# Order of weight casts, a scan product, the last sums and the output rows in a two-layer hybrid decoder trunk

## The chip, the cores and the metric

The kernel is one program on one core of a Trainium2 chip. The core has five engines, each with its own instruction queue: TensorE (PE; its weight loads are a row of their own, PEld), VectorE (DVE), ScalarE (ACT), GpSimd (POOL) and SyncE (SP), which here only issues DMAs. An engine works its queue in order, and an instruction waits in its queue until what it needs is there. The metric is device time in microseconds (us) from the first to the last instruction of one launch; lower is better.

## What is computed

`x` has 512 positions of width 1024. There are two layers, each a "macaron": half a SwiGLU feed-forward (FFN), a mixer, half a SwiGLU again, each on an RMS-normalised input. The mixer is a Mamba-2 SSD in layer 0 and an S5 state space model in layer 1. A last RMSNorm gives the output.

```python
for i in range(2):
    x = x + 0.5 * swiglu(rmsnorm(x, ffn1_norm[i]), ffn1_w_in[i], ffn1_w_out[i])   # inner width 2816
    h = rmsnorm(x, mix_norm[i])
    x = x + (ssd_mixer(h, ...) if i == 0 else s5_mixer(h, ...))
    x = x + 0.5 * swiglu(rmsnorm(x, ffn2_norm[i]), ffn2_w_in[i], ffn2_w_out[i])
return rmsnorm(x, final_norm)
```

The S5 mixer has 64 groups of 16 channels with 64 complex states each: a product into the states, a linear recurrence over time, a product back, a gelu, and a gated linear unit (GLU) with a 1024 x 2048 weight. Everything is float32.

## The kernel before

**Stages.** `STAGES` is `f1_0`, `ssd`, `f2_0`, `f1_1`, `s5`, `f2_1`. The residual is kept transposed, eight tiles `xT[0..7]` of 128 channels x 512 positions. `f1_0` uses `ffn`; the other three feed-forwards use `ffn7`.

**Three products for one.** Each fp32 operand is split into a rounded high half and the rest: ACT casts the high half (`whi`, L226), DVE subtracts to get the low half (`wlo`, L228), and `proj` (L235 to L237) adds high x high, high x low and low x high in PSUM. `split_w` does both halves of a weight tile; `split(j)` calls it for the j-th weight of an `ffn7` stage, `fetch_to(j)` sends its DMA on SP.

**The end of an `ffn7` stage.** The 22 blocks of the inner width are worked in five parts, and after each part eight output tiles d = 0..7 are accumulated (`part`, 15 matmuls of 512 columns for a part of five blocks). `after(d)` then adds the product to the residual on DVE (L594 or L597, here "the add of tile d"), and in the last part starts the next norm: `nxt.take(d)` has ACT square the tile (L160) and, where the next stage is a feed-forward, make its high half `hH` (L173); `rest` has DVE make `hL` (L182) and add the square to `acc` (L167). `rest` of tile d is held in `held` until tile d+1. After the last tile, `nxt.sums()` sums `acc` and the last square over the partitions on PE (L198 for S5, L137 otherwise), and `finish()` runs the Newton iterations for 1/sqrt on DVE (L121 to L128). For the last stage, `fin_sink` has ACT scale a tile (L1592); its `rows` turns it on PE (L1597) and copies it to `fo` on DVE (L1598). At most three `rows` wait in `later`; `flush` runs them.

**Lists of work between.** `fill` holds functions that `ffn7` calls one by one, one after each block and after each `after(d)`. In `f1_1`, entries 54 to 61 fall to d = 0..7 and the last, 62, behind them. They load what the S5 stage needs, and `res_w(j)` casts the first four GLU weights (ACT L1381, DVE L1389; weight j loaded by `res_load(j)`, L1375).

**Order.** `tc.manual_schedule(engines=...)` keeps the named engines in the order of the program; where nothing is named, a planner places an engine's instructions by its own simulation of the times. Inside `ffn7` nearly everything is in program order on all engines (`ALL`), but each call is a region of its own; the planner may still place instructions of one region among those of the next. In `s5_stage` PE, SP and POOL are in program order, DVE and ACT are the planner's.

**The S5 stage** works eight blocks of eight groups. `states(i)` scales the input tile `U` by the norm on DVE (L1407) and multiplies it into PSUM on PE (L1413); `swap(i)` copies it half by half on ACT (L1424, L1425); `scan(i)` is eight steps on DVE (L1433 to L1445, with the recurrence at L1437) with two ACT copies in the middle (L1441, L1442) and gives `v`. `mix(i, h, 128)` and `mix(i, h, 0)` multiply `U` and `v` of blocks i and i+1 back (L1454). `channels(i)` turns and splits the gelu's result (L1474 on PE, L1478 on ACT, L1479 on DVE), and `glu_k(k)` accumulates its part of the first four GLU columns, which needs `res_w(0..3)`. `aux` PSUM has four slots, `mm` four.

**The output.** Each of four blocks of 128 rows is scaled by the norm (ACT L1767 or DVE L1765) and sent as one DMA (L1768).

## Time and profile before

| | |
|---|---|
| median of 3 runs | 2044.01 us (2043.23 to 2044.3) |
| profiled execution: its own time | 2039.9 us |
| its span, first to last instruction | 2038.0 us |
| mean granted TensorE clock | 0.991 of full speed |
| busy: PE, PEld, DVE, ACT, POOL | 1988.1, 1727.5, 1493.7, 943.4, 223.9 us |
| PE waiting, named waits above 1 us each, between 1500 and 1700 us | 22.7 us |
| DMA | 265.47 MB, mean 130 GB/s |

The profile is of one execution. A row of its timeline has the start, the duration, the engine, the line of the kernel, the operation, output and inputs, and in brackets how long the engine sat idle before it and what ended that. Matmuls overlap, so their durations are longer than their spacing.

### The profile page before, as it was taken

To read this page: it belongs to the slowest core of one execution; us is meant where nothing else is said; L and a number is where in the kernel's file an instruction comes from. 1 tells how busy PE (TensorE), PEld (TensorE's weight loads), DVE (VectorE), ACT (ScalarE), POOL (GpSimd) and SP (SyncE) were. 2 spreads that over 40 slices of the span, in tenths; PEclk is the share of its full clock that TensorE was granted. 3 is DMA by queue.
4 is the path that set the end of the run, shared out by engine and by line. 5 is a ranking of instruction groups with operands and counts; after the bars stand their busy time and mean duration, and the time that the engine had idled before them with its cause. 6 is when DMAs were issued, how large, how long until landed. Compare 5 with 4: busy or idle time off the path is not lost. (4 is left out here: it accounts for less than half of the span.)

```text
span 2038.0 us, 32117 instructions
## 1 busy us (share of the span) xinstructions
PE 1988.1 (98%) x12477; PEld 1727.5 (85%) x12477; DVE 1493.7 (73%) x2677; ACT 943.4 (46%) x1613; POOL 223.9 (11%) x338
## 2 busy tenths in 40 slices
PE   8999999999999999999999999999996999999997
PEld 7887778888888887889999978999985888999996
DVE  6899995688885787776677677677768657866675
ACT  5324334465663555434444534454444433444453
POOL 1002332012111010000111000001101100100010
PEclk9999999999999999999999999999997999999999
DMA  7436676344333332455566336446767432654561
GB/s 183 127 120 170 161 193 136 93 113 125 110 107 112 99 93 62 115 133 119 138 152 151 86 92 157 114 124 147 177 184 259 134 95 80 163 136 114 129 142 66
DMA packets 410057, 265.47 MB, mean 130 GB/s; under 512 B 40008, under 2 KB 383088, under 8 KB 409904
## 3 DMA queue, kind: packets, MB, share of 16 engines
q1 hardware_dynamic: 383024, 202.60, 35.5%
q0 software_dynamic: 26560, 59.75, 14.1%
q8 instruction: 98, 1.61, 0.3%
q10 hardware_dynamic: 320, 1.06, 0.1%
q14 instruction: 55, 0.45, 0.1%
HBM read 215.06 MB, written 21.04 MB: 116 GB/s over the span
## 5 line engine op out<-in xcount | busy, mean ns | idle before, releaser
L226 ACT CAST whi<-wst 128x1024 fp32r<-128x1024 f32 (+3 forms) x354 | 315.5, 893 | 373.7 <-PE mm L236 290.6
L228 DVE TENSOR_TENSOR wlo<-wst,whi 128x1024 fp32r<-128x1024 f32 (+3 forms) x354 | 364.1, 1029 | 120.8 <-ACT whi L226 119.0
L235 PE MATMUL mm<-hH,whi 128*128 128x512 f32 x984 | 389.9, 396 | 0.0
L236 PE MATMUL mm<-hL,whi 128*128 128x512 f32 x984 | 384.8, 391 | 1.8 <-DVE hL L182 1.7
L237 PE MATMUL mm<-hH,wlo 128*128 128x512 f32 x984 | 383.8, 390 | 0.0
L237 PE MATMUL mm<-ah,wlo 128*128 128x512 f32 x704 | 274.8, 390 | 0.0
L235 PE MATMUL mm<-ah,whi 128*128 128x512 f32 x704 | 274.5, 391 | 0.0
L236 PE MATMUL mm<-al,whi 128*128 128x512 f32 x704 | 274.4, 390 | 0.0
L236 PEld LDWEIGHTS mm<-hL,whi 128*128 128x128 f32 x984 | 185.1, 188 | 40.8 <-DVE hL L182 3.0
L235 PEld LDWEIGHTS mm<-hH,whi 128*128 128x128 f32 x984 | 185.0, 188 | 39.8 <-issue 1.8
L237 PEld LDWEIGHTS mm<-hH,wlo 128*128 128x128 f32 x984 | 185.0, 188 | 39.5 <-issue 0.4
L384 PE MATMUL mm<-th,hH 128*128 128x256 f32 x612 | 173.5, 284 | 0.0
L386 PE MATMUL mm<-th,hL 128*128 128x256 f32 x612 | 173.2, 283 | 0.0
L385 PE MATMUL mm<-tl,hH 128*128 128x256 f32 x612 | 173.1, 283 | 0.0
L237 PEld LDWEIGHTS mm<-ah,wlo 128*128 128x128 f32 x704 | 132.2, 188 | 28.0 <-issue 0.6
L236 PEld LDWEIGHTS mm<-al,whi 128*128 128x128 f32 x704 | 132.3, 188 | 26.5 <-issue 0.2
L235 PEld LDWEIGHTS mm<-ah,whi 128*128 128x128 f32 x704 | 132.3, 188 | 26.1
L299 POOL DMA_DIRECT2D wu<-wst x51 | 43.1, 846 | 827.5 <-DMA wst<-in_ffn_w_in_dram 384.4
L384 PEld LDWEIGHTS mm<-th,hH 128*128 128x128 f32 x612 | 117.4, 192 | 2.4 <-ACT up L458 2.4
L385 PEld LDWEIGHTS mm<-tl,hH 128*128 128x128 f32 x612 | 117.4, 192 | 0.0
L386 PEld LDWEIGHTS mm<-th,hL 128*128 128x128 f32 x612 | 117.4, 192 | 0.0
L385 PE MATMUL mm<-tl,whi 128*128 128x256 f32 x408 | 115.5, 283 | 0.0
(393 smaller groups left out, 3917.6 us busy)
## 6 DMA issues: line engine op xcount, KB each, us to landing
wst<-in_ffn_w_in_dram SPq DMA_DIRECT2D x125, 512.0 KB, 4.6
wu<-in_ffn_w_in_dram SPq DMA_DIRECT2D x51, 512.0 KB, 5.9
wst<-in_ssd_in_proj_dram SPq DMA_DIRECT2D x48, 512.0 KB, 4.0
wst<-in_ffn_w_out_dram SPq DMA_DIRECT2D x72, 256.0 KB, 2.9
wst<-in_ffn_w_out_dram SPq DMA_DIRECT2D x48, 320.0 KB, 3.2
wu<-wst POOLq DMA_DIRECT2D x51, 256.0 KB, 4.5
ws<-wst POOLq DMA_DIRECT2D x51, 256.0 KB, 4.8
dec<-d_cs POOLq DMA_DIRECT2D x16, 512.0 KB, 4.8
```

The lines of the kernel that those rows point to most:

```text
L226: S.copy(hi, st)
L228: V.tensor_tensor(lo, st, hi.bitcast(F32), op=OP.subtract)
L235: PE.matmul(ps, hi[:, k], H[k], start=first and k == 0, stop=False)
L236: PE.matmul(ps, hi[:, k], L[k], start=False, stop=False)
L237: PE.matmul(ps, lo[:, k], H[k], start=False, stop=last and k == n - 1)
L299: G.dma_start(dst, src, accum_op=OP.add)
L384: PE.matmul(ps[:, c0], hi[:, k], mh, start=first and k == 0, stop=False, skip_group_check=True)
L385: PE.matmul(ps[:, c0], hi[:, k], ml, start=False, stop=False, skip_group_check=True)
L386: PE.matmul(ps[:, c0], lo[:, k], mh, start=False, stop=k == 3, skip_group_check=True)
```

## The change

- `split` becomes `high` (fetch and ACT cast) and `low` (DVE subtraction). In the last part of an `ffn7` stage the ACT cast of a coming weight is issued ahead of the tile's square as before, but its DVE subtraction comes behind the add of the tile; at d = 0 and 1 one weight each is cast, so two by d = 1 where there was one.
- In `f1_1`, `rest` of tile 6 (its square into `acc`) comes ahead of the add of tile 7.
- After the last tile, all but the last `rows` are flushed, then the sums are issued, then the last `rows`.
- `res_w(3)` leaves the `fill` list of `f1_1` and stands in `s5_stage` behind `scan(1)`, where ACT and DVE are the planner's.
- `states(3)` is issued ahead of `mix(0, h, 0)`.
- `f2_0` and `f1_1` together lie in one region that keeps all engines in program order.
- The last two of the eight final tiles are copied from PSUM by ACT.
- The output is scaled and sent in eight blocks of 128 half rows (128 x 512): n = 1, 4, 7 scaled and issued by ACT, the other five scaled by DVE and issued by SP.

```diff
-    def split_w(st, kt):
+    def split_hi(st, kt):
         hi = wpool.tile([128, KD, 128], F32R, name="whi", bufs=3)[:, :kt]
         S.copy(hi, st)
+        return hi
+
+    def split_lo(st, hi, kt):
         lo = wpool.tile([128, KD, 128], F32R, name="wlo", bufs=3)[:, :kt]
         V.tensor_tensor(lo, st, hi.bitcast(F32), op=OP.subtract)
         return hi, lo
...
+        halves = {}
+
+        def high(j):
+            if j < len(items) and j not in whole and j not in halves:
+                fetch_to(j)
+                halves[j] = split_hi(raws[j], items[j][1])
+
+        def low(j):
+            if j in halves:
+                whole[j] = split_lo(raws[j], halves.pop(j), items[j][1])
...
-                def after(d):
+                def after(d, j=None):
                     pops(1)
+                    if d == KD - 1 and last and turn:
+                        held.pop(0)()
...
                     if last:
                         held.append(nxt.take(d, hold=True))
-                        if d:
+                        low(j)
+                        if len(held) > 1:
                             held.pop(0)()
...
-                        split(j + 2)
-                        fetch_to(j + 5)
+                        if not last:
+                            split(j + 2)
+                            fetch_to(j + 5)
                         for e in range(2):
-                            after(e)
+                            high(j + 2 + e)
+                            if e == 0:
+                                fetch_to(j + 5)
+                            after(e, j + 2 + e)
                         continue
                     part(d, 0, n)
-                    if d < KD - 1 or last:
+                    if last:
+                        high(j + 2)
+                    elif d < KD - 1:
                         split(j + 2)
                     fetch_to(j + 5)
-                    after(d)
+                    after(d, j + 2)
...
+            nxt.flush(1)
+            if nxt.kind != "hilo":
+                nxt.sums()
             nxt.flush()
             if nxt.kind != "hilo":
-                nxt.sums()
                 nxt.finish()
...
             scan(1)
+            res_w(3)
...
             states(2)
+            states(3)
             for h in range(2):
                 mix(0, h, 0)
-            states(3)
...
-            V.tensor_copy(fin["o"][:, :, d * 128:(d + 1) * 128], p.rearrange("p (t c) -> p t c", t=4))
+            o, pv = fin["o"][:, :, d * 128:(d + 1) * 128], p.rearrange("p (t c) -> p t c", t=4)
+            if d < KD - 2:
+                V.tensor_copy(o, pv)
+            else:
+                S.copy(o, pv)
...
             elif s in s5_pre:
+                region.enter_context(tc.manual_schedule(engines=ALL))
                 with tc.manual_schedule(engines=MAN):
...
-                fill = [lambda: None] * 63
+                fill = [lambda: None] * 62
...
-                fill[62] = lambda: res_w(3)
...
                          have=have, turn=lambda: s5["op"].tile([128, T], F32, name="xn", bufs=1))
+                region.close()
             else:
...
-    for t in range(4):
-        if t % 2:
-            V.tensor_scalar(fin["o"][:, t], fin["o"][:, t], prep.y4[:, t:t + 1], None, op0=OP.mult)
+    for n in range(8):
+        t, cs = n // 2, slice(n % 2 * 512, n % 2 * 512 + 512)
+        o, y, dst = fin["o"][:, t, cs], prep.y4[:, t:t + 1], out[0, t * 128:(t + 1) * 128, cs]
+        if n % 3 == 1:
+            S.activation(o, o, AF.Copy, scale=y)
+            nc.scalar.dma_start(dst, o)
         else:
-            S.activation(fin["o"][:, t], fin["o"][:, t], AF.Copy, scale=prep.y4[:, t:t + 1])
-        (nc.sync, nc.scalar)[t % 2].dma_start(out[0, t * 128:(t + 1) * 128, :], fin["o"][:, t])
+            V.tensor_scalar(o, o, y, None, op0=OP.mult)
+            nc.sync.dma_start(dst, o)
```

More of the change, by code (lines that the diff above doesn't have):

```diff
@@ L229, in split_w @@
         return hi, lo
+    def split_w(st, kt):
+        return split_lo(st, split_hi(st, kt), kt)
     def proj(ps, w, H, L, first=True, last=True):
@@ L327, in fetch_to @@
                 raws.append(fetch_w(*items[len(raws)])[0])
+        halves = {}
[6 more added lines that the diff above has]
+                whole[j] = split_lo(raws[j], halves.pop(j), items[j][1])
         def split(j):
-            if j < len(items) and j not in whole:
-                fetch_to(j)
-                whole[j] = split_w(raws[j], items[j][1])
+            high(j)
+            low(j)
         sevens = list(range(parts[0][1], FT))
@@ L599, in after @@
                         held.append(nxt.take(d, hold=True))
-                        if d:
+                        low(j)
+                        if len(held) > 1:
                             held.pop(0)()
@@ L1597, in rows @@
                 PE.transpose(p[:, t * 128:(t + 1) * 128], xg[:, t * 128:(t + 1) * 128], ident)
-            V.tensor_copy(fin["o"][:, :, d * 128:(d + 1) * 128], p.rearrange("p (t c) -> p t c", t=4))
+            o, pv = fin["o"][:, :, d * 128:(d + 1) * 128], p.rearrange("p (t c) -> p t c", t=4)
[3 more added lines that the diff above has]
+                S.copy(o, pv)
         return rows
-    op_es = ExitStack()
+    op_es, region = ExitStack(), ExitStack()
     def prep_for(st):
```

## The prediction, made before the changed kernel was run

> **What bounds the kernel now.** I read the page first: the busy shares and the two rows of slices for PE and its clock.
>
> ```profile
> PE 1988.1 (98%) x12477; PEld 1727.5 (85%) x12477; DVE 1493.7 (73%) x2677; ACT 943.4 (46%) x1613; POOL 223.9 (11%) x338
> PE   8999999999999999999999999999996999999997
> PEclk9999999999999999999999999999997999999999
> ```
>
> PE is the bound nearly everywhere. The exceptions are slice 30 (1528 to 1579 us), the S5 scans, where the clock falls too, and the last slice. Work on DVE or ACT is worth something only where PE or the end waits for it, so I asked next for PE's waits: first at the join of `f2_0` and `f1_1` (1100 to 1300), then around S5 (1480 to 1720).
>
> ```profile
> PE mm L236 <- DVE hL L182: 1.4, 1, 1.4
> ...
> PE aux L1454 <- DVE v L1445: 12.4, 4, 4.9
> PE aux L1413 <- DVE U L1407: 5.8, 1, 5.8
> PE aux L1454 <- issue: 2.3, 1, 2.3
> PE aux L198 <- POOL v L1440: 2.2, 1, 2.2
> ```
>
> Together with the output's tail, these places are all that this change can shorten; the other weight casts that it moves stand beside a PE that waits for nothing. The sum is made against the profiled execution, 2039.9 us (span 2038.0, 1.9 around it); it lies 4.1 below the median of 2044.0. I subtract the gain from the median.
>
> **Term 1, the join of f2_0 and f1_1.** Timeline of DVE and PE:
>
> ```profile
> 1179.76 0.69 DVE L597 SCALAR_TENSOR_TENSOR xT<-mm,xT 128x512 f32<-128x512 f32 x1
> 1181.62 1.22 DVE L228 TENSOR_TENSOR wlo<-wst,whi 128x1024 fp32r<-128x1024 f32 x1
> 1182.75 0.75 DVE L182 SCALAR_TENSOR_TENSOR hL<-xT,cols,hH 128x512 fp32r<-128x512 f32 x1
> 1183.55 0.50 PE L236 MATMUL mm<-hL,whi 128*128 128x512 f32 x1 [1.42 <-DVE hL L182]
> ```
>
> PE waits 1.42 for the last `hL`, which stands behind a weight subtraction that begins 1.13 earlier (1181.62 to 1182.75). That subtraction is `f1_1`'s own third weight, put ahead by the planner. One region over both stages forbids it: -1.13 alone. With the adds ahead of the subtractions, the add at 1179.76 also comes sooner, so the whole wait goes: **-1.4** (ends 0 and -1.4). Next late would be tile 6's `hL`, now done before PE asks. The displaced subtraction serves a weight that is used behind two whole projections of 24 matmuls, which cover it; uncovered it would cost its 1.22. SP's order is the same in both programs.
>
> **Term 2, the sums before S5.** Timeline of the end of `f1_1`, DVE, ACT, PE:
>
> ```profile
> 1527.15 0.79 DVE L167 TENSOR_TENSOR acc<-acc,sq 128x512 f32<-128x512 f32 x1
> 1528.57 1.29 DVE L1389 TENSOR_TENSOR hL<-wst,hH 128x512 fp32r<-128x512 f32 x2 [0.63 <-ACT hH L1381]
> 1532.51 1.29 DVE L1389 TENSOR_TENSOR hL<-wst,hH 128x512 fp32r<-128x512 f32 x2 [2.64 <-ACT hH L1381]
> 1533.72 0.22 DVE L121 TENSOR_SCALAR nw_v<-aux 128x64 f32<-128x64 f32 x1
> 1536.87 2.50 DVE L1407 TENSOR_TENSOR U<-U,nw_y 128x512 f32<-128x512 f32 x4
> ...
> 1527.40 0.63 ACT L160 ACTIVATE sq<-xT 128x512 f32<-128x512 f32 x1 [0.84 <-DVE xT L594]
> 1531.86 1.14 ACT L1381 CAST hH<-wst 128x512 fp32r<-128x512 f32 x2 [2.80 <-DMA wst<-in_s_glu_w_dram]
> ...
> 1528.05 1.97 PE L198 MATMUL aux<-acc,sel 128*128 128x64 f32 x16 [2.16 <-POOL v L1440]
> 1529.85 1.95 PE L198 MATMUL aux<-sq,sel 128*128 128x64 f32 x16
> ```
>
> PE is free at 1525.89 (1528.05 less 2.16) and starts when `acc` holds tile 6 (1527.15 + 0.79 = 1527.94). The wait's named releaser, a POOL memset, is not what the code makes it wait for. With tile 6's square ahead of the add of tile 7, and the adds no longer behind subtractions, `acc` is ready before PE is. The 1.80 of the first sums (1528.05 to 1529.85) then falls into the wait for the last square, done at 1528.03; the second sums run 1528.05 to 1530.0. The Newton steps, though, started only at 1533.72, behind `res_w(3)`, whose weight landed at about 1531.8. With `res_w(3)` gone they start at 1530.05; `res_w(2)` (done 1529.86) still fits before. That is **-3.7**. The ends: -0 if something takes `res_w(3)`'s place, -3.7. I take the latter, since in the program nothing stands between the sums and Newton.
>
> `res_w(3)` itself, two ACT casts (1.14) and two DVE subtractions (1.29), is not saved. It has room on ACT under Newton, and on DVE behind the first two of the four scalings of `U` (1536.87, 0.6 each), where 1.48 stood idle before 1540.84 (below). I take 0; without that cover it is +1.2 on DVE.
>
> **Term 3, the fourth scan product.** PE, then DVE, then groups of DVE lines between 1530 and 1600, then SP:
>
> ```profile
> 1568.86 1.73 PE L1454 MATMUL aux<-opP,v 128*64 128x128 f32 x13 [2.81 <-DVE v L1445]
> 1572.11 1.13 PE L1454 MATMUL aux<-opP,v 128*64 128x128 f32 x15
> ...
> 1540.84 0.69 DVE L1433 TENSOR_TENSOR z<-aux,tb 128x512 f32<-128x512 f32 x1 [1.48 <-ACT z L1425]
> 1560.22 0.69 DVE L1433 TENSOR_TENSOR z<-aux,tb 128x512 f32<-128x512 f32 x1 [3.44 <-ACT z L1425]
> ...
> L1433 DVE TENSOR_TENSOR z<-aux,tb 128x512 f32<-128x512 f32 x8 | 5.5, 687 | 5.9 <-ACT z L1425 5.9
> L1444 DVE TENSOR_TENSOR z<-z,tb 128x504 f32<-128x504 f32 x8 | 5.4, 680 | 1.3 <-ACT z L1442 1.1
> ...
> 1539.63 0.32 SPq L1340 DMA_DIRECT2D opH<-d_H  x1
> ```
>
> In this stretch DVE sets the pace: PE's four waits at L1454 are for its `v`. DVE itself idles 3.44 before scan 3, because `states(3)` stood behind `mix(0, h, 0)`, which waited for scan 1. Issued ahead, it needs the PSUM slot that scan 1's first step frees, `U(3)` (scaled by 1539.4), and an operator whose DMA SP issues at 1539.63. DVE then goes from scan 2 into scan 3 without the gap, and PE's resumption at 1568.86, after which it hardly waits again, moves with it: **-3.4** (ends 0 and -5.9, all of L1433's idle). `mix(0, h, 0)` now queues behind `states(3)`; it waited for scan 1 anyway. SP and POOL keep their order.
>
> **Term 4, the tail.** DVE, ACT, PE, and one microsecond of the windows (DMA share, GB/s last):
>
> ```profile
> 2024.67 2.48 DVE L1598 COPY fo<-aux 128x512 f32<-128x512 f32 x4
> 2027.06 0.15 DVE L121 TENSOR_SCALAR nw_v<-aux 128x4 f32<-128x4 f32 x1
> 2029.50 1.42 DVE L1765 TENSOR_SCALAR fo<-fo,nw_y 128x1024 f32<-128x1024 f32 x2
> 2024.25 0.63 ACT L160 ACTIVATE sq<-xT 128x512 f32<-128x512 f32 x1 [2.63 <-DVE xT L597]
> 2030.29 0.37 ACTq L1768 DMA_DIRECT2D out_dram<-fo  x1
> 2026.13 0.43 PE L137 MATMUL aux<-ones,acc 128*32 128x1 f32 x32
> 2026.40 0.44 PE L137 MATMUL aux<-ones,sq 128*32 128x1 f32 x32
> 2031.00:2032.00 1.00, 0.00 (x0) 0.00 (x0) 0.00 (x0) 0.69 (x1) 0.00 (x0) 0.50 0.89 348
> ```
>
> The sums take 0.71 and can start after the last square (2024.88): done at 2025.65. DVE has two copies left instead of four, 0.6 each, free at about 2025.9. Newton starts there instead of 2027.06: -1.15. The two copies on ACT run beside Newton's 2.44 (2027.06 to 2029.50). Half rows are scaled some 0.35 sooner than whole ones (1.42 / 2 = 0.71 for a whole one), so the first DMA leaves that much sooner: -0.35. Data flows from about 2031.1, 0.8 behind that issue, at 348 GB/s in 0.89 of a microsecond, 391; 2.1 MB at that rate take 5.4, as before, and the last issue comes well within that. Term 4 is **-1.5** (ends -0.5, if smaller transfers flow worse, and -1.7).
>
> Beside this stands a rule that speaks against it. The Trainium skill, "DMA: Bandwidth & Descriptors", section "Anatomy of one DMA", gives each DMA about 2.0 us fixed plus its bytes at 436 GB/s; one after another, eight transfers of 256 KB would be 21 us where four of 512 KB are 13, an estimate from that page that would make this term +6.5. The window above, at 391 GB/s with several in flight, speaks against taking them singly.
>
> **Sum:** -1.4 - 3.7 - 3.4 - 1.5 = -10.0, so 2034.0 us (2029.9 for an execution like the profiled one).
>
> **Rivals.** *Newton stays blocked (2037.7).* `res_w(3)` is now the planner's to place. If its simulation has the weight landing early, DVE gets those subtractions into the small hole before Newton (1529.86 to 1530.05) and waits for the real landing at 1531.8: term 2 is gone, 2044.0 - 6.3. For it: four scalings of `U` already run well ahead of their place in the program. Against it: Newton is ready almost at once.
>
> *The S5 gains are swallowed (2041.1).* If DVE's new order, or loads that cannot come sooner, give back terms 2 and 3, only 1.4 + 1.5 = 2.9 stay. For it: one load waited on a full queue in this stretch.
>
> ```profile
> 1559.11 6.89 SPq L1340 DMA_DIRECT2D opH<-d_H  x1
> ```
>
> Against it: that load is for blocks used 20 us later.
>
> *The clock too (2032.7).* The windows show PE at 0.50 from 1566 to 1572, after a wait of 2.81:
>
> ```profile
> 1568.00:1569.00 1.00, 0.14 (x2) 0.17 (x4) 1.00 (x3) 0.96 (x3) 0.00 (x0) 0.50 0.97 381
> ...
> 1582.51 1.04 PE L1454 MATMUL aux<-opP,v 128*64 128x128 f32 x16
> ```
>
> The products from 1568.86 to 1573.24, three groups of thirteen to fifteen, took 4.4; sixteen at full clock take 1.04, so 3.1 for three. If the shorter wait keeps the clock up, 1.3 more goes. The Trainium skill, "TensorE: Matmul & The Clock Gate", section "What's actually happening", says that a free-running window of 3.4 us decides, so a mostly idle window halves the clock and a busy one restores it; the halved stretch here, about two such windows, agrees. Against it: DVE would then be late again.
>
> *The drain (2039.6).* If each of the eight transfers showed its 0.8 of start-up, where one shows it now, 5.6 would be added. For it: smaller pieces. Against it: the rate with four in flight.
>
> *Slower (2050).* The planner stops weaving the scans.
>
> ```profile
> 1565.57 0.61 ACT L1441 COPY z<-z 64x504 f32<-64x504 f32 x1 [1.74 <-DVE z L1437]
> ```
>
> Each scan has two pauses of two such copies on ACT, 2.4 in all, 19.5 for eight (an estimate from this row), of which 7.2 are paid now (5.9 + 1.3 above). Bare, they cost +12.3, against -6.6 from terms 1, 2 and 4: +5.7. It turns slower once the bare pauses pass 13.8 in all, about six of the eight scans. For it: DVE and ACT are free here and their inputs move. Against it: the weave now leaves only 7.2.
>
> **How the numbers follow.** Chances: forecast 0.41, Newton blocked 0.25, swallowed 0.16, clock 0.07, drain 0.02, slower 0.09. About 4 us (0.2%) is what a measurement of this kernel can tell from no change. Faster: 0.41 + 0.25 + 0.07 + 0.02 = 0.75; same 0.16; slower 0.09. The range from 2031.5 (clock case, and a little of L1433's other idle) to 2041.5 (swallowed) leaves out the slower case and some of each end.
>
> **What would show it.** Right: no wait at L236 near 1180; Newton's first step within 0.2 us of the sums' end; `states(3)` directly behind `states(2)` and no 3 us gap before scan 3; Newton at the end about 2.4 us behind the last add, and output at 400 GB/s. Wrong: L1389 between the sums and Newton, DVE idle inside the scans above 7 us, PE's waits at L1454 still near 12, or output below 300 GB/s. The blocked rival would show in the DVE order alone; the slower one only in many short waits for ACT.

## The result and the profile after

The changed kernel is faster: median 2032.69 us (2031.72 to 2034.68, 4 executions) beside 2043.62 for the kernel before (2040.74 to 2044.3, 4 executions), a ratio of 0.995 with a 95% interval of 0.9934 to 0.9966. The forecast was 2034.0 with a range of 2031.5 to 2041.5. The profiled execution took 2032.91 (span 2031.1), 6.9 less span than the profiled one of before. The medians differ by 10.9. Those two differences do not agree, and most of the experiments go into that.

The page's busy shares and the rows of slices, the same three as before:

```profile
PE 1987.0 (98%) x12477; PEld 1727.1 (85%) x12477; DVE 1493.0 (74%) x2678; ACT 944.6 (47%) x1616; POOL 225.6 (11%) x338
PE   8999999999999999999999999999996999999997
PEclk9999999999999999999999999999997999999999
```

Nothing is to be seen at this scale. PE is busy 1.1 us less, and slice 30 still reads 6. The waits of PE, from 1480 to 1720, changed in kind (engine, line, releaser: us in total, times, longest):

```profile
PE aux L1481 <- DVE v L1472: 7.5, 4, 3.7
PE aux L1440 <- DVE U L1434: 6.8, 1, 6.8
PE aux L1440 <- issue: 2.6, 1, 2.6
PE aux L1481 <- issue: 1.5, 1, 1.5
PE aux L1501 <- ACT gy L1489: 0.7, 1, 0.7
PE mm L242 <- DVE hL L182: 0.3, 1, 0.3
```

Lines have moved by 27 in the S5 stage: L1481 is the old L1454 (products back), L1440 the old L1413 (`states`), L1472 and L1471 the old L1445 and L1444 (`v`), L1460 the old L1433 (first step of a scan), L1416 and L1408 the two halves of `res_w`. The wait for `v` fell from 12.4 to 7.5, and the 2.2 ahead of the sums is gone. Others are new or longer: 1.0 more for `U`, 2.6 at `states`, 0.7 for `gy`. All in all 19.4 against 23.0 (the 22.7 of the table before, and a 0.3 for `hL` that stood there too).

**The join.** DVE's timeline at the end of `f2_0`, then the first and the last of seven starts of PE there now, and the first, second and last of the same seven before:

```profile
1179.02 0.75 DVE L182 SCALAR_TENSOR_TENSOR hL<-xT,cols,hH 128x512 fp32r<-128x512 f32 x1
1180.28 0.75 DVE L182 SCALAR_TENSOR_TENSOR hL<-xT,cols,hH 128x512 fp32r<-128x512 f32 x1
1180.94 1.22 DVE L231 TENSOR_TENSOR wlo<-wst,whi 128x1024 fp32r<-128x1024 f32 x1
...
1181.16 0.39 PE L241 MATMUL mm<-hH,whi 128*128 128x512 f32 x1
1182.61 0.43 PE L137 MATMUL aux<-ones,acc 128*32 128x1 f32 x32
...
1180.68 0.39 PE L235 MATMUL mm<-hH,whi 128*128 128x512 f32 x1
1181.15 0.50 PE L236 MATMUL mm<-hL,whi 128*128 128x512 f32 x1
1184.22 0.43 PE L137 MATMUL aux<-ones,acc 128*32 128x1 f32 x32
```

The last `hL` now stands ahead of the weight subtraction (L231), and PE has no wait at all between 1100 and 1300. The six matmuls ahead of the sums (L137) take 1.45 from start to start (1181.16 to 1182.61) where they took 3.54 (1180.68 to 1184.22).

**The end of f1_1.** Timeline of DVE, ACT and PE:

```profile
1530.00 0.69 DVE L1416 TENSOR_TENSOR hL<-wst,hH 128x512 fp32r<-128x512 f32 x1 [2.05 <-ACT hH L1408]
1530.61 0.22 DVE L121 TENSOR_SCALAR nw_v<-aux 128x64 f32<-128x64 f32 x1
1530.74 0.68 DVE L1416 TENSOR_TENSOR hL<-wst,hH 128x512 fp32r<-128x512 f32 x1
1531.34 0.19 DVE L122 TENSOR_SCALAR nw_h<-nw_v 128x64 f32<-128x64 f32 x1
1529.35 1.14 ACT L1408 CAST hH<-wst 128x512 fp32r<-128x512 f32 x2 [2.20 <-DMA wst<-in_s_glu_w_dram]
1524.13 1.89 PE L198 MATMUL aux<-acc,sel 128*128 128x64 f32 x16
1526.17 2.00 PE L198 MATMUL aux<-sq,sel 128*128 128x64 f32 x16
```

The sums start without a wait and end at 1528.17. The Newton steps (`nw_v`) could start there, but start at 1530.61: DVE stood 2.05 us at a subtraction of `res_w(3)`, whose weight had not landed (ACT's cast of it waited 2.20 for the DMA). The second half of the same subtraction cuts in behind Newton's first step. This is what the forecast called "Newton stays blocked", here for 2.4 us.

**The scans.** The two groups of DVE that had 5.9 and 1.3 us of idle time before (between 1530 and 1600; here between 1527 and 1594), then two rows of DVE's and one of PE's timeline:

```profile
L1460 DVE TENSOR_TENSOR z<-aux,tb 128x512 f32<-128x512 f32 x8 | 5.5, 685 | 2.2 <-ACT z L1452 2.2
L1471 DVE TENSOR_TENSOR z<-z,tb 128x504 f32<-128x504 f32 x8 | 5.4, 681 | 2.5 <-ACT z L1469 2.4
...
1543.06 0.68 DVE L1460 TENSOR_TENSOR z<-aux,tb 128x512 f32<-128x512 f32 x1
1554.26 0.68 DVE L1460 TENSOR_TENSOR z<-aux,tb 128x512 f32<-128x512 f32 x1
1543.84 1.15 PE L1440 MATMUL aux<-U,opH 128*64 128x64 f32 x32 [2.62 <-issue]
```

Scan 3 starts at 1554.26 with no idle time before it, where 3.44 stood. `states(3)` (1543.84) waits 2.62 on PE. The profile names no releaser; it starts 0.1 behind the end of scan 1's first step (1543.06 + 0.68), which frees the PSUM slot that it needs by the code. L1460's idle fell by 3.7 and L1471's grew by 1.2, so 2.5 net.

**The tail.** DVE, ACT, SP, and two of the microseconds of output (share of DMA and GB/s last), then two of those of the kernel before:

```profile
2019.17 1.28 DVE L1628 COPY fo<-aux 128x512 f32<-128x512 f32 x2
2020.37 0.15 DVE L121 TENSOR_SCALAR nw_v<-aux 128x4 f32<-128x4 f32 x1
2020.74 0.59 ACT L1630 COPY fo<-aux 128x512 f32<-128x512 f32 x1 [0.28 <-PE aux L1625]
2023.36 3.74 SPq L1804 DMA_DIRECT2D out_dram<-fo  x5
...
2025.00:2026.00 1.00, 0.00 (x0) 0.00 (x0) 0.00 (x0) 0.00 (x0) 0.00 (x0) 0.50 1.00 367
2026.00:2027.00 1.00, 0.00 (x0) 0.00 (x0) 0.00 (x0) 0.00 (x0) 0.00 (x0) 0.50 1.05 387
...
2033.00:2034.00 1.00, 0.00 (x0) 0.00 (x0) 0.00 (x0) 0.00 (x0) 0.00 (x0) 0.50 1.01 393
2034.00:2035.00 1.00, 0.00 (x0) 0.00 (x0) 0.00 (x0) 0.00 (x0) 0.00 (x0) 0.50 1.02 410
```

Newton starts behind two copies, ACT does the other two beside it, and eight transfers of 256 KB flow at 367 to 387 GB/s in the four whole microseconds of output. The four of 512 KB before flowed at 393 to 410 (2032 to 2036), so the smaller ones are about 6% slower, some 0.35 us for the 2.1 MB (an estimate from these rates).

**A ruler for small effects.** Executions of one kernel differ by several us, more than most of the terms. Each stage that ends in a norm has a first Newton step (`nw_v`), and the times between these split an execution into pieces, of which only those that an edit touches should move. In the table, the columns are the first Newton step behind `f2_0`'s start, the length from there to the steps of `f1_1`, S5, `f2_1` and the last norm, and from there to the end:

| kernel | start | f2_0 and join | f1_1 | S5 | f2_1 | end | span |
|---|---|---|---|---|---|---|---|
| before | 837.18 | 349.18 | 347.36 | 148.32 | 345.02 | 10.94 | 2038.0 |
| before, run again | 835.63 | 349.13 | 348.76 | 148.80 | 345.02 | 10.96 | 2038.3 |
| changed | 837.66 | 347.10 | 345.85 | 145.93 | 343.83 | 10.73 | 2031.1 |
| changed, run again | 836.25 | 347.09 | 345.81 | 145.91 | 343.82 | 10.72 | 2029.6 |

The pieces repeat within 0.1 us, but for two in the kernel before (f1_1 and S5) and the start, which moves by 1.4 to 1.6 in either kernel. In the kernel before that is a half clock of 3.4 us from 790 on (1.7 us lost), which all of the fourteen profiles of this document show but the second one of before; in the kernel changed both profiles have it, and the 1.4 is not explained. From the first row to the third: +0.5 - 2.1 - 1.5 - 2.4 - 1.2 - 0.2 = -6.9.

### The profile page after: what moved, and what is told of

The parts are those of the page before. It is cut to its first block, busy times and chain, and to the rows that moved or that the text cites. A ratio compares the mean times of both kernels' runs of the same rounds, so it can differ in the third digit from the quotient of the medians.

```text
span 2031.1 us, 32128 instructions
## 1 busy us (share of the span) xinstructions
PE 1987.0 (98%) x12477; PEld 1727.1 (85%) x12477; DVE 1493.0 (74%) x2678; ACT 944.6 (47%) x1616; POOL 225.6 (11%) x338
## 4 chain that ended last, share of the span: by engine, by line
PE 57%; DVE 2%; ACT 1%; issue 1%; DMA 0%; DVEq 0%; SPq 0%; ACTq 0%
PE mm L241 10%; PE mm L242 10%; PE mm L243 10%; PE mm L400 6%; PE mm L401 6%; PE mm L402 6%; PE aux L402 2%; PE aux L401 2%; PE aux L400 2%; DVE z L1464 0%; PE aux L242 0%; PE aux L243 0%; PE aux L241 0%; DMA wst<-in_s_glu_w_dram 0%; PE aux L1481 0%
## 5 line engine op out<-in xcount | busy, mean ns | idle before, releaser
L231 DVE TENSOR_TENSOR wlo<-wst,whi 128x1024 fp32r<-128x1024 f32 (+3 forms) x354 | 363.9, 1028 | 98.6 <-ACT whi L226 96.8
L615 DVE SCALAR_TENSOR_TENSOR xT<-mm,xT 128x512 f32<-128x512 f32 x112 | 77.1, 688 | 65.4 <-PE mm L243 65.3
```

The source lines that it names most:

```text
L231: V.tensor_tensor(lo, st, hi.bitcast(F32), op=OP.subtract)
L615: V.scalar_tensor_tensor(xT[d], pos[d], 0.5, xT[d], op0=OP.mult, op1=OP.add)
```

## The experiments

All comparisons have five rounds. The median, the range and the count of executions are of the kernel named; the ratio is to the kernel before, run beside it. The comparisons were made in three sets, by the record on three different chips, so differences between medians of different sets say less than the ratios and the pieces.

### Does the kernel before have one time?

**The kernel before, unchanged, as a kernel of its own** (no edit).

> The kernel before, unchanged, as a second look. Between the two profiled executions the change gains 6.9 us of span (2038.0 to 2031.1), between the medians 10.9 (2043.62 to 2032.69). Theory A: the executions of before simply scatter, its profiled one (2039.9) lies at the fast end, and no stage of its own explains the difference: a second profile has the same waits within 0.5 us each, and the median over more runs comes out at 2041 to 2043, so that the change is worth 8 to 9. Theory B: the slower executions of before have one place that is longer (the S5 stage, where PE waits and the granted clock halves): a second profile near 2043 would show 3 to 4 us more in the waits at the scans than the first, and the median stays at 2043 to 2044.

Measured: 2040.55 (2039.0 to 2043.69, 11), ratio 0.9998 [0.9989, 1.0007]. The bound of 0.2% for what counts as a change holds. The median lies below what either theory gave, that of the 25 executions beside it (2041.52) in the range of theory A. The single times are not spread evenly, though. As the other side of the comparisons of all the sections here, the kernel before ran 66 times: 34 executions lie between 2037.62 and 2041.56 (median 2040.05), 32 between 2042.57 and 2044.30 (median 2043.45), none between. The step is 3.4. Of the eleven executions of this section, eight lie in the lower group, two in the upper one, and one (2042.16) in the gap, so the gap is thin but not empty. The execution profiled first (2039.9) is of the lower group, the median of 2044.01 that the forecast subtracted from is of the upper.

In this run's profile the sums of `f1_1` took nearly twice the 1.97 and 1.95 shown before (PE, then DVE):

```profile
1526.42 3.65 PE L198 MATMUL aux<-acc,sel 128*128 128x64 f32 x16 [2.16 <-POOL v L1440]
1529.86 3.62 PE L198 MATMUL aux<-sq,sel 128*128 128x64 f32 x16
1533.52 0.22 DVE L121 TENSOR_SCALAR nw_v<-aux 128x64 f32<-128x64 f32 x1 [1.86 <-PE aux L198]
```

Newton then waits for the sums (1.86) and no longer for `res_w(3)`. So the granted clock had halved in the 2.16 wait ahead of the sums in this execution, and not in the first. S5, where theory B looked for the difference, is 0.5 longer here, not 3 to 4.

### The join

**The region alone.** The kernel before with `f2_0` and `f1_1` in one region, nothing else.

```diff
             elif s in s5_pre:
+                region.enter_context(tc.manual_schedule(engines=ALL))
...
+                region.close()
```

> Before, with f2_0 and f1_1 in one region that keeps all engines in program order, and nothing else. Theory A (the planner's early subtraction alone made PE wait for the last hL): the wait of 1.42 falls to 0.3 or less, 1.1 to 1.4 us faster (ratio 0.9993 to 0.9995). Rival B (the adds ahead of the subtractions did it): the wait stays above 1, no change. If the region also moves other work in the planner's order, the time may differ by several us either way.

Measured: 2036.8 (2035.69 to 2037.56, 9), ratio 0.9975 [0.9965, 0.9984]. The wait at the join falls to 0.30 and the piece "f2_0 and join" to 348.0, 1.2 less, both as expected. The median is 4.7 less than that of before beside it, which misses the expected 1.1 to 1.4 and is more than the wait can give. Its nine executions lie within 1.9 of each other, with no second group.

**The wait kept, and filled.** In the kernel before, six matmuls whose result nobody uses are put where PE waits for `hL`.

```diff
+                        hi, lo = whole[0]
+                        proj(pg, (hi[:, :7], lo[:, :7]), pr.H[:7], pr.L[:7], last=False)
+                        idle = aux_ps()
+                        for n in range(6):
+                            PE.matmul(idle, hi[:, n], pr.H[n], start=n == 0, stop=n == 5)
+                        proj(pg, (hi[:, 7:], lo[:, 7:]), pr.H[7:], pr.L[7:], first=False)
```

> Before, with six extra matmuls of 512 columns (1.4 us by the 0.23 spacing; their PSUM is never read) put into PE's wait for the last hL at the join of f2_0 and f1_1. The wait is filled, not removed; nothing downstream starts earlier. Theory A (a wait of this length lets the granted clock halve in part of the executions, 3.4 us lost each time, as in the profile of the fourth-product run at 1183 to 1191): the median falls by 1.5 to 3.4 us against before although no wait is gone (ratio 0.9985 to 0.9993), and no execution shows a halved clock at the join. Rival B (the join costs its 1.4 of waiting and nothing else, and the region's 4.7 came from another order of work): no change, or up to 0.3 us slower.

Measured: 2039.73 (2037.73 to 2041.35, 11), ratio 0.9992 [0.9983, 1.0001]. The wait still costs its time (the piece is 349.14), the lowest times are those of before, and the upper group is gone: 0 of 11. The interval of the ratio reaches 1, so it is the missing group, more than the median, that speaks for theory A.

**Both waits filled**, the join's and the 2.16 ahead of the sums, with nine more such matmuls there.

```diff
+                for n in range(9):
+                    PE.matmul(idle, h[:, n % 5], AH[n % 5], start=n == 0, stop=n == 8)
             if nxt.kind != "hilo":
                 nxt.sums()
```

> Before, with extra matmuls in two waits: six at the join of f2_0 and f1_1, nine (2.1 us) ahead of the sums before S5. Nothing starts earlier by itself. Theory A (the clock halves in these two waits in part of the executions): the sums take 1.9 to 2.0 a half in every execution instead of up to 3.65, no halved stretch stands at the join, the median falls to 2038 to 2039.5, near the fastest executions of before (2037.6), and none is above 2041. Rival B (the scatter of before is loads landing late): spread and median as before, 2040.5 to 2042.

Measured: 2039.51 (2038.28 to 2041.08, 11), ratio 0.999 [0.9981, 0.9998]. Again none of the upper group: with the run before, 0 of 22, where the kernel before has 32 of 66. The sums take 1.97 and 1.95 in its profile, where they took 2.52 and 3.62 with the join's wait alone filled. By the medians, filling that second wait gives nothing on top (2039.51 beside 2039.73); by the pieces f1_1 is 0.8 shorter (346.81 beside 347.60), and no more, since Newton then stands behind `res_w(3)`.

What the upper group is can be read where a profile happened to catch the clock at the join. Single microseconds there (PE's busy time and matmuls first, the granted clock third from the right), of the fourth product alone (below):

```profile
1182.00:1183.00 1.00, 0.00 (x0) 0.00 (x0) 1.00 (x2) 0.00 (x0) 0.00 (x0) 1.00 0.37 111
1183.00:1184.00 1.00, 0.94 (x11) 0.43 (x14) 0.00 (x1) 0.37 (x1) 0.00 (x0) 0.74 0.30 81
1184.00:1185.00 1.00, 1.00 (x65) 0.98 (x65) 0.29 (x1) 0.68 (x1) 0.00 (x0) 0.50 1.09 329
...
1189.00:1190.00 1.00, 1.00 (x4) 0.81 (x3) 0.00 (x0) 0.00 (x0) 0.00 (x0) 0.50 0.02 6
```

and of the kernel before, run again:

```profile
1184.00:1185.00 1.00, 1.00 (x7) 0.80 (x6) 0.96 (x3) 0.00 (x0) 0.00 (x0) 1.00 0.38 102
1189.00:1190.00 1.00, 1.00 (x8) 0.87 (x7) 0.00 (x0) 0.53 (x1) 0.00 (x0) 1.00 0.00 0
```

The same wait of 1.4 us halves the clock behind it in one execution (full matmuls fall from 6 to 8 a microsecond to 4) and not in the other. From 1183 to 1191 the loss is 3.4 us of full clock, summed from the rows (1 less the clock in each): the step between the two groups. The execution profiled for `res_w(3)` alone (below), at 2042.7 in the upper group, also has the clock at 0.50 there, and in these two profiles the f1_1 piece is 350.79 and 350.84, 3.4 more than the 347.36 of the first profile. That the wait at the join can cost 3.4 us is shown by these two profiles, and that it makes the upper group, by the 22 executions in which filling it removes that group.

The traces also show much of what decides in a single execution. In each of them the granted clock changes only at moments that lie whole multiples of 3.41 us apart. In the first profile it is halved from 1534.54 to 1541.37, from 1548.19 to 1558.43 and from 1565.26 to 1572.09: two, three and two times 3.41, with two times 3.41 between them. (In a row of one microsecond such a moment shows as a mixed value: the 0.74 of 1183 above puts it at 1183.5.) Where these moments fall against the program differs from execution to execution. Counted on to the join, one of them cuts the wait in the two profiles that kept the clock (1182.96 in a wait from 1182.13 to 1183.55, 1181.51 in one from 1180.53 to 1181.97), and none does in the two that lost it: 1180.06 and 1183.47 around a wait from 1181.62 to 1183.06, 1179.58 and 1182.99 around one from 1181.18 to 1182.62. Four executions are few, and the uncut length of a wait is not the whole rule: ahead of the sums an uncut 1.82 (1525.89 to 1527.71) kept the clock in the first profile, where 1.44 lost it at the join.

### The sums and Newton

**The casts alone.** The new order of casts, adds and squares in the feed-forwards, without the region, `res_w(3)`, `states(3)` and the tail (in the kernel changed, these are put back).

```diff
-                region.enter_context(tc.manual_schedule(engines=ALL))
...
-            res_w(3)
...
-            states(3)
             for h in range(2):
                 mix(0, h, 0)
+            states(3)
...
+                fill[62] = lambda: res_w(3)
```

> Before, with the weight subtractions behind the adds and tile 6's square ahead of the add of tile 7, and nothing else (no region, res_w(3) in its old place, old order of states(3), old tail). The wait of 2.16 ahead of the sums before S5 should go, so that the sums end about 2 us sooner and never run at a halved clock (3.6 a half instead of 1.95). Theory A (Newton is then held by the fourth GLU weight, which lands when it lands): under 1.5 us of that reaches the end where the weight is late, and what is gained is mostly clock; the join's wait shrinks by less than 0.5; 0.5 to 2.5 us faster in all (ratio 0.9988 to 0.9998). Rival B (the order of casts is what the change lives on): 4 us or more.

Measured: 2035.59 (2035.13 to 2036.35, 6), ratio 0.997 [0.9958, 0.9981]: 5.8 less, beyond the 0.5 to 2.5 that the waits as first profiled allow, and of the size that the other theory gave. The pieces: 347.32 (-1.9), 346.07 (-1.3), 147.37 (-1.0). The edit by itself takes the join's wait away, like the region does, and with it the upper group, which the expectation (less than 0.5 off that wait) did not foresee; and the sums have no wait ahead and run in 1.89 and 2.00.

**`res_w(3)` alone.** The kernel before, with `res_w(3)` moved behind `states(0)` and `states(1)`, its subtractions held there.

```diff
+            res_w(3, pin=True)
...
-                fill[62] = lambda: res_w(3)
```

> Before, with res_w(3) pinned behind the first two scalings of U, and nothing else. Theory A (term 2 needs both: here the sums still end late): Newton starts right behind the sums, which end at about 1531.8 at full clock and 1533.5 at half, so 1.9 us is gained at most and nothing where the sums ran at half clock; 0.3 to 1.9 faster in the median (ratio 0.9991 to 0.9998). Rival B (the landing of the fourth weight alone held S5): 2.5 us or more faster.

Measured: 2040.62 (2037.34 to 2044.22, 11), ratio 0.9996 [0.9987, 1.0005]; 5 of 11 in the upper group. No gain. PE and DVE show why:

```profile
1530.11 2.70 PE L198 MATMUL aux<-acc,sel 128*128 128x64 f32 x16 [2.16 <-POOL v L1442]
1532.60 3.62 PE L198 MATMUL aux<-sq,sel 128*128 128x64 f32 x16
1536.26 0.23 DVE L121 TENSOR_SCALAR nw_v<-aux 128x64 f32<-128x64 f32 x1 [4.34 <-PE aux L198]
```

Newton is free of `res_w(3)` and, in this execution, waits 4.34 for the sums, which run largely at half clock behind their 2.16 wait. Each of the two delays can cover the other; both have to be taken away.

**Newton freed in the kernel changed.** There the planner is kept from moving `res_w(3)`: it is called behind `states(0)` and `states(1)`, and its subtractions stay in the order of the program.

```diff
             scan(1)
-            res_w(3)
...
             for i in range(2):
                 states(i)
+            res_w(3, pin=True)
             for h in range(2):
                 mix(0, h, 128)
...
+            if pin:
+                tc.keep_in_program_order(ins)
```

> The changed kernel with res_w(3) called behind the scalings of U for blocks 0 and 1 and its DVE part pinned behind them in DVE's order, so that nothing stands between the sums and the Newton steps. Theory A (the half subtraction that the planner put ahead of Newton held it until the fourth GLU weight landed): Newton's first step moves from 2.4 us behind the sums' end to under 0.2 us, the end of Newton comes 2.9 us sooner, and the kernel is 2.5 to 3 us faster than the changed one (about 2030, ratio to before about 0.9935). Rival B (the S5 stage is then held by loads): the first scan starts 2.9 sooner, but PE waits for operators later in the stage, and at most 1 us is left at the end (2032).

Measured: 2029.09 (2028.57 to 2030.37, 5), ratio 0.9939 [0.9926, 0.9951], 2.8 to 3.6 less than the two medians of the changed kernel, as theory A expected or a little more. DVE:

```profile
1528.09 0.22 DVE L121 TENSOR_SCALAR nw_v<-aux 128x64 f32<-128x64 f32 x1 [0.26 <-PE aux L198]
1531.24 1.29 DVE L1436 TENSOR_TENSOR U<-U,nw_y 128x512 f32<-128x512 f32 x2
1532.45 1.28 DVE L1416 TENSOR_TENSOR hL<-wst,hH 128x512 fp32r<-128x512 f32 x2
```

Newton starts right behind the sums. The f1_1 piece is 343.42, 2.4 less than in the changed kernel and 3.9 less than before, the 3.7 that the forecast took for it. `res_w(3)`'s subtractions stand between two scalings of `U` and delay nothing: the S5 piece is 144.64, 1.3 less than in the changed kernel.

**Newton's wait filled.** The same kernel with 15 matmuls for nobody behind the sums.

```diff
+            if turn:
+                h, lo = whole[at[len(parts) - 1, KD - 1]]
+                idle = mm_ps()
+                for n in range(15):
+                    PE.matmul(idle, h[:, n % 5], AH[n % 5], start=n == 0, stop=n == 14)
             nxt.flush()
```

> The kernel with Newton freed (2029.1), with fifteen extra matmuls of 512 columns (3.4 us) behind the sums, in PE's wait of 3.9 us for the Newton steps; their PSUM is never read. Theory A (the clock is halved when PE resumes, so that the 64 products of states(0) and states(1) take 3.6 instead of 2.1): the products run at full clock, the first scan starts 0.8 sooner and the second copy 1.5 sooner, 0.8 to 1.5 us faster than without (about 2028). Rival B (DVE's chain sets the pace behind the first scan, whatever the clock): the first scan starts 0.8 sooner and the end gains under 0.5. If the extra work delays PE, 0.5 slower.

Measured: 2027.47 (2027.14 to 2028.6, 5), ratio 0.9932 [0.9919, 0.9944], the fastest of all. PE:

```profile
1526.90 3.67 PE L682 MATMUL mm<-ah,whi 128*128 128x512 f32 x15
1531.04 2.16 PE L1447 MATMUL aux<-U,opH 128*64 128x64 f32 x64 [0.46 <-DVE U L1441]
```

`states(0)` and `states(1)`, 64 matmuls, take 2.16 instead of 3.68 at the place where the last kernel's PE had waited 3.94. Part of what that wins is given back: the half clock comes later in the scans, and the S5 piece is 143.95, 0.7 less. The medians, from two sets, differ by 1.6; 0.9 of the same difference between the two profiles lies in the start, which the edit does not touch.

### The fourth scan product

**Alone**, in the kernel before:

```diff
             states(2)
+            states(3)
             for h in range(2):
                 mix(0, h, 0)
-            states(3)
```

> Before, with states(3) issued ahead of mix(0, h, 0), and nothing else. Theory A (term 3 stands by itself): DVE's idle of 3.4 before scan 3 goes, the scans from there on come 3 to 3.4 us sooner, the kernel is 3 us faster (ratio 0.9985). Rival B (much of the 10.9 hangs on this move, since in before's slower executions PE and the clock lose more here): 5 us or more faster. Rival C: the planner's other order for DVE eats the gain, under 1 us.

Measured: 2038.84 (2037.1 to 2040.13, 11), ratio 0.9988 [0.9979, 0.9997]. DVE's idle ahead of scan 3 is gone, and the S5 piece is 144.68, 3.6 less than before; its profile has the clock halved at the join, so that its span (2037.3) shows little of that. The eleven executions lie within 3.0 of each other and do not form two groups, although the join's wait (1.44) stands in this kernel too. By the account above two groups were to be expected; why there are none is open.

**Taken out of the changed kernel**, the opposite edit:

```diff
             states(2)
-            states(3)
             for h in range(2):
                 mix(0, h, 0)
+            states(3)
```

> The changed kernel with states(3) back behind mix(0, h, 0). Theory A (term 3 stands beside the others): DVE's idle before scan 3 is back at 3 to 3.5, S5 from its Newton to the next norm takes 147 to 148.5 instead of 145.9, 2 to 3 us slower than the changed kernel. Rival B (with the other waits gone the scans are not what PE waits for): under 1 us slower.

Measured: 2035.67 (2034.15 to 2036.31, 5), ratio 0.9963 [0.995, 0.9975], 3.8 more than the changed kernel beside it (2031.9). The S5 piece is 147.68, 1.8 more, the f1_1 piece 0.7 more, and PE's waits for `v` are 10.3 (four) where the changed kernel has 7.5:

```profile
PE aux L1481 <- DVE v L1472: 10.3, 4, 4.0
```

DVE's idle ahead of scan 3 comes back as 1.19 only, not as the 3 to 3.5 expected. That idle time was 3.44 in the first profile of before, 2.86 in the second, 2.06 with the region alone and 1.31 with the casts alone, so the other parts of the change had already shortened it. This part brings 1.8 to 3.6 in the piece that it touches; the rest of the 3.8 lies in the f1_1 piece and in the start.

### The tail

**The old tail in the changed kernel**: last sums behind all `rows`, four copies on DVE, four whole rows of output.

```diff
-            nxt.flush(1)
...
-            if d < KD - 2:
-                V.tensor_copy(o, pv)
-            else:
-                S.copy(o, pv)
+            V.tensor_copy(o, pv)
...
-    for n in range(8):
+    for t in range(4):
```

> The changed kernel with the tail of before: sums behind all turns, all final copies on DVE, four whole-row outputs. Theory A (term 4 stands by itself): 1.4 us slower than the changed kernel's span at the end, Newton 1.2 later and the output 0.2 longer (ratio to before about 0.9962 where the changed kernel has 0.9955). Rival B (the smaller transfers flow worse and give the gain back): within 0.4 us of the changed kernel.

Measured: 2032.89 (2032.14 to 2034.97, 5), ratio 0.9959 [0.9946, 0.9971]. By the medians the old tail costs 0.2 (beside 2032.69) or 1.0 (beside 2031.9 in another comparison), by the ratios about 2, with intervals that overlap. By the pieces the new tail is worth what was forecast: 345.01 and 10.94 here, as in the kernel before, against 343.83 and 10.73, so 1.2 + 0.2 = 1.4. This execution's start was 1.1 sooner than that of the changed one (836.55 against 837.66) and its S5 piece 0.4 shorter, which hides it in the span. That the medians hold 1.4 as well was not shown.

**The changed kernel once more.**

> The changed kernel, unchanged, beside more executions of before. Theory A (before's executions scatter because the clock halves at the join and at the sums in part of them, the changed kernel's do not): its executions lie within 3 us of each other where before's spread over 5 to 6, median 2032 to 2033.5 against 2041 to 2042, ratio 0.9955 to 0.996. Rival B (the 10.9 of the first comparison is the gain): ratio 0.995 or less.

Measured: 2031.9 (2031.08 to 2034.25, 5), ratio 0.9948 [0.9935, 0.996]. Newton stands behind half of `res_w(3)` again (2.01 idle on DVE), so this is the plan of the kernel and not an accident of one execution. The executions lie within 3.2 of each other, as expected; the ratio is that of rival B, not the 0.9955 to 0.996 of theory A.

## Why the prediction was right

The time (2034.0) was 1.3 from the measured one, and "faster" held. The sum of terms, -10.0, lies beside -10.9 and -9.0 in the two comparisons. It is right partly because two errors cancel. By the terms:

| term | forecast | pieces, profile to profile | what the experiments add |
|---|---|---|---|
| 1, join | -1.4 | -2.1 | -1.2 for the region alone, -1.9 for the casts alone; 3.4 more in the executions of the upper group |
| 2, sums and Newton | -3.7 | -1.5 | -3.9 once Newton is freed |
| 3, fourth product | -3.4 | -2.4 | -3.6 alone, 1.8 when taken back |
| 4, tail | -1.5 | -1.4 | the same by the pieces |

**Term 1** had the mechanism and not the whole price. The wait at L236 went, as forecast, and either edit takes it, or most of it; what the two give is not additive. Of the -2.1, 1.42 is the wait. The rest lies in the starts beside it: tile 6's product came 0.47 behind its predecessor instead of 0.23 (1181.15), since its `hL` was late too (the working names it and gives it no price), and the starts behind each pause cost some 0.1 more; from 1180.68 to the sums that is 3.54 against 1.45. What was left out is the clock: the working counts it only as a rival inside S5, and only from one profile in which the join happened to keep it. With 32 of 66 executions in the upper group, this is 3.4 x 32 / 66 = 1.6 in the mean, and all of 3.4 for a median that lies in it. The rule of the Trainium skill that the working cites for S5 ("TensorE: Matmul & The Clock Gate", section "What's actually happening") bears on this place too. It names an idle window of about 3.4 us; "mostly idle" is the working's own word. The traces agree in the 3.41 us between possible changes, and differ in that a wait of 1.44, less than half of such a window, was enough in two profiles; the measurement decides.

**Term 2** was mis-sized, by 2.2. The failing step is the sentence "I take the latter, since in the program nothing stands between the sums and Newton". On DVE the order of the program is not the order of the engine: the planner set half a subtraction of `res_w(3)` ahead of Newton, as the rival *Newton stays blocked* said, and its weight landed late, as that rival said too. The rival had 0.25 and a price of the whole 3.7; it came true for 2.2. The 1.5 that did come is not the work of the earlier sums. These end 2.0 sooner against the first Newton step of `f1_1` (1531.80 - 1186.36 before, 1528.17 - 1184.76 now), but in neither profile did Newton wait for them. It is that one half of the subtraction stands ahead of Newton where both did (0.6), and that the weight landed 0.9 sooner by the same measure (ACT's cast at 1531.86 before, 1529.35 now). That the sums wait for nothing, the first half of the step, held; so did one sign named for being wrong, L1389 (now L1416) between the sums and Newton. The cover claimed for the displaced `res_w(3)` also held, where it stands behind Newton: 1.28 between two scalings, and a shorter S5 piece.

**Term 3** held in its mechanism, and was mis-sized by 1.0. Scan 3 follows scan 2 with no gap, and L1460's idle fell by 3.7. The step that missed is that nothing takes the place: DVE now has 1.2 more idle time inside the scans, at L1471, behind ACT's copies, and 3.7 - 1.2 = 2.5 is what the S5 piece lost (2.4). `mix(0, h, 0)` behind `states(3)` cost what was said: its first products waited only for `v`.

Of *The clock too*, one half came about. From 1540 to 1594 (clock third from the right), before and changed:

```profile
1540.00:1560.00 20.00, 10.87 (x166) 10.15 (x164) 15.50 (x21) 9.01 (x15) 2.83 (x8) 0.71 0.83 261
1560.00:1594.00 34.00, 28.35 (x346) 24.87 (x348) 30.87 (x48) 18.89 (x36) 6.73 (x14) 0.90 0.81 274
```

```profile
1540.00:1560.00 20.00, 12.30 (x188) 10.99 (x186) 18.88 (x29) 9.86 (x17) 3.40 (x8) 0.66 0.91 295
1560.00:1594.00 34.00, 29.34 (x325) 25.35 (x321) 29.56 (x45) 19.65 (x35) 10.01 (x17) 1.00 0.86 278
```

The halved stretch around 1570 is gone (0.90 to 1.00 over 34 us, 3.4 us of full clock), but ahead of it more is halved (1545 to 1559, 6.8 where 5.1 were), which leaves 1.7. It is not counted beside term 3, since DVE sets the pace there; that no part of it reached the end was not shown. The rival also read its row too late: the half clock began at 1565.26 (the microsecond from 1565 reads 0.63), before the wait of 2.81 (1566.06 to 1568.86), so that wait did not bring it on.

**Term 4** held, -1.4 for -1.5: Newton 1.2 sooner, the output 0.2 instead of 0.35. (By its own rows the sums were to end at 2025.59, not 2025.65; nothing hangs on it.) The rule on fixed costs per DMA, weighed there at +6.5, does not bind: eight transfers in flight ran at 367 to 387 GB/s. In the Trainium skill the section cited gives that rule for DMAs that GpSimd issues; here SP and ACT issue them, before and after. The rate was not "as before", though, nor the 400 named as a sign: it is about 6% below the 393 to 410 of before, a small part of the low end that the term had allowed for.

**The sum.** Terms 2 and 3 brought 3.2 less than forecast. Term 1 brought 0.7 more. The clock at the join, in no term, brought 3.4 where the median of before lay in the upper group, as in the comparison first run. That the total came out near is therefore in good part luck. From the lower group's median (2040.05) to the median of all nine executions of the changed kernel (2032.47) it is 7.6, near the 6.9 of the profiles. The step that hid this is the first of the working: the gain was sized in a profile that was 4.1 below the median and subtracted from the median, as if the 4.1 were an offset that every execution has. By the groups, those 4.1 are mostly the join's 3.4, in the very place that the change mends; the executions of that median were not profiled.

Two differences between pieces can be traced. The S5 piece of the region alone is 1.4 shorter than before (146.92): the region also changed the planner's order on DVE, so that the last step of scan 1's `v` (L1445) stands 10.65 behind scan 0's first step (1549.48 - 1538.83) instead of 12.21 (1553.05 - 1540.84), `mix(0, h, 0)` and `states(3)` come sooner, and DVE idles 2.06 ahead of scan 3 instead of 3.44. The f1_1 piece of before is 1.4 longer in its second profile: the half clock at the sums held Newton for 1.86, while the weight of `res_w(3)` landed 0.55 sooner. Not settled are the 1.4 between the starts of the changed kernel, and the lack of two groups in the fourth product alone.

## What to carry to other kernels

When a profiled execution lies some us off the median, look at the single times first: two groups, 3.4 us apart here, mean that a place in the kernel can go either way, and a short wait of PE is a first suspect; filling it with matmuls that nobody reads tests that and may itself pay (0.7 us by the pieces in the fastest version). Work that a planner may place, and whose input is a DMA, wants to be pinned behind the step that must not wait, since the planner's idea of when the load lands may be too early. Short effects are read from the time between fixed steps of one execution, most of which repeated within 0.1 us here, not from medians that move by 2.

## What was not expected of the hardware

A wait of PE of 1.4 us, with a busy PE on both sides, halved the granted clock behind it in two profiles, at 3.4 us of full clock each, and left it up in two others; with six matmuls in the wait none of 22 executions lay in the upper group. In the four profiles with this wait the clock fell where the wait lay whole between two of the moments, 3.41 us apart, at which it can change. A wait of 2.16 ahead of 32 small matmuls did the same to these (3.65 and 3.62 instead of 1.97 and 1.95). And eight output transfers of 256 KB flowed at 367 to 387 GB/s, about 6% below the 393 to 410 of four of 512 KB, so that halving them cost some 0.35 us by these rates.
